# An encoder layer on one core: q stored in rows of 4 KB, the second chunk's tiles in another order, and VectorE's list of the first wave rearranged

## The chip, the cores and the metric

The kernel runs on one core of one Trainium2 chip. The metric is device microseconds for one execution. Everything is float32; matrix products keep their accuracy by splitting each operand into a high and a low half (type fp32r) and adding three products.

## The reference

One transformer layer with window attention and a dense feed-forward part, for one sequence of 2048 tokens and 1024 features:

```python
mod = silu(c) @ ada_w + ada_b                # 48 tiles of 128 values
sh1, sc1, g1, sh2, sc2, g2 = split(mod, 6)
h = rmsnorm(x, mix_norm_pre) * (1 + sc1) + sh1
q, k, v = split(h @ w_qkv)                   # 16 q heads, 4 k and v heads, 64 wide
logits = q @ k_band / 8 + rel_bias           # a block of 128 queries, 384 keys, |distance| <= 128
y = softmax([logits, sink])[..., :-1] @ v_band
x = x + g1 * rmsnorm(y @ w_o, mix_norm_post)
h = rmsnorm(x, ffn_norm_pre) * (1 + sc2) + sh2
a, b = split(h @ ffn_w_in)
x = x + g2 * rmsnorm((silu(a) * b) @ ffn_w_out, ffn_norm_post)
```

## The kernel before

**Chunks and tiles.** The tokens are cut into four chunks of 512. A chunk's x lies as eight tiles `x0` to `x7` of 128 features x 512 tokens (in the rows `x1_5` is chunk 1's tile 5). From them come a norm (`squares`, `norm`) and, for each k of eight, a scaling (`scale`, L207, written over x) and the two halves of `h` (`halves`: the high half on ScalarE, L214, the low half on VectorE, L215). The eight x buffers are shared, so a chunk's x tile is loaded when the low half of the chunk before it is done. The twelve output tiles of a chunk are numbered 0 to 7 for q, 8 and 9 for k, 10 and 11 for v; each is 24 matmuls (8 k, three products by the helper `three`, L145 to L147) of 128 x 512 into one of eight PSUM buffers. `NORD = [8, 9, 0, 1, 2, 3, 4, 10, 11, 5, 6, 7]` is their order in the weights: the first seven (`NORD[:WAVE]`) read the weight slices `w1`, the last five `w2`.

**The first wave** computes chunk 0's first seven tiles together, k by k, as the weights arrive. For each k VectorE has two adaLN products (`ada_reduce`, L297: a 128 x 1024 tile of `ada_w` times the conditioning vector, summed; tile 8+k gives the scale for x, tile k the shift for h), the low half of a weight slice (L151), a scaling and a low half of h. `squares0` squares chunk 0's x on ScalarE and adds pairs on VectorE; TensorE sums the four that are left over the partitions (`nsta`, L121). `tc.issue_after(...)` bounds from when on the scheduler may place what stands under it.

**Chunk 0's rest and chunk 1.** Then come the two v tiles (`psv`) and q tiles 5 to 7 of chunk 0, which read `w2` (loaded by `w_piece(k, 1)` through four raw buffers, cast on ScalarE, split on GpSimd), the norm of chunk 1 after the v tiles (`nsta`, L127, from the halves `nhla`, which take a buffer that the v tiles' stores give back), and chunk 1's twelve tiles. `late_ada` loads the 24 adaLN tiles that the attention doesn't need yet and reduces them between these. `evac` empties a q tile: high half on ScalarE (L229), low half on VectorE (L230), and for two tiles four DMA stores to the DRAM tensor `q_d` (L235), issued on ScalarE's queue for chunks 0 and 1 and on SP's after that. Loads and other stores are issued by SP, in order.

**Attention** has 64 units of 128 queries and four heads. `load_qkv` fetches q, k and v of a chunk and a k/v head. A unit has four score products (`s`, L497; the 128 x 128 piece of q is the weight operand, loaded anew for each of the two halves of k), the softmax on VectorE, ScalarE and GpSimd, transpositions (`t`, L519) and products with v. Chunks 2 and 3's projections and the output projection fill TensorE between the units. The memory of `w1`, `w2` and the raw buffers is used again for q, k, v and the softmax, from its beginning on: q, k and v lie where `w1` was.

**Feed-forward.** The hidden values come in pairs of blocks, whose sums and differences `give_pair` makes and stores; in the second half they are split before they are stored (`parted`). Instructions are ordered by a scheduler that has a timeline model; code order and `issue_after` guide it.

Of the kernel before, what the change touches and what calls it, by code (L numbers as in the profile page):

```python
# [10 lines left out]
F32 = mybir.dt.float32  # L11
F32R = mybir.dt.float32r
AF = mybir.ActivationFunctionType
ALU = mybir.AluOpType
# [3 lines left out]
P = 128  # L18
# [4 lines left out]
NCH = S // CH  # L23
NB = S // P
JB = CH // P
HEADS = 16
KVH = 4
GRP = 4
DH = 64
# [10 lines left out]
QW = P // GRP  # L40
# [4 lines left out]
NORD = [8, 9, 0, 1, 2, 3, 4, 10, 11, 5, 6, 7]  # L45
WAVE = 7
# [16 lines left out]
def f(ap):  # L63
    return ap.bitcast(F32)
# [3 lines left out]
def encoder_layer(ctx, tc, a):  # L68
# [9 lines left out]
    const = open_pool(ctx, "const")  # L78
    dram = open_pool(ctx, "dram", space=DRAM)

    q_d = [[dram.tile([P, JB * GRP, P], F32, name=f"q_d{c}_{g}") for g in range(KVH)] for c in range(NCH)]
    k_d = [[dram.tile([P, 2, CH], F32, name=f"k_d{c}_{g}") for g in range(KVH)] for c in range(NCH)]
    v_d = [[dram.tile([P, JB, P], F32, name=f"v_d{c}_{g}") for g in range(KVH)] for c in range(NCH)]
    o_d = [[dram.tile([P, KT, P], F32, name=f"o_d{c}_{b}") for b in range(JB)] for c in range(NCH)]
# [83 lines left out]
    class Chunk:  # L168
# [20 lines left out]
        def squares0(self):  # L189

            sq = [ev.tile([P, GRP, CH], F32, tag="eq", name=f"nsq0_{i}", bufs=2) for i in range(2)]
            sq = [sq[k // GRP][:, k % GRP] for k in range(KT)]
            for k in range(KT):
                act.activation(sq[k], self.xt[k], AF.Square)
                if k % 2:
                    dve.tensor_tensor(sq[k - 1], sq[k - 1], sq[k], ALU.add)
            self.acc = sq[::2]

        def norm(self, psp, ptag):
            self.r = rstd_of(lambda name: square_at(), psp, ptag, self.acc, f"a{self.c}", normed[:, 3])  # L200
# [18 lines left out]
    def evac(c, n, ps, psp, ptag):  # L219

        if n < KT:
            g, e = n // 2, n % 2
            if (c, g) not in pairs:
                pairs[c, g] = ev.tile([P, 2, JB * GRP, 2, QW], F32R, tag="eq", name=f"eq{c}_{g}", bufs=2)
            t = pairs[c, g]

            hi, lo = (t[:, i, :, e, :].rearrange("p (b s) r -> p b s r", b=JB) for i in range(2))
            src = ps.rearrange("p (b t) -> p b t", t=P)[:, :, ::-1].rearrange("p b (s r) -> p b s r", r=QW)
            act.activation(hi, src, AF.Copy, scale=DH ** -0.5)  # L229
            newest["evac"] = dve.scalar_tensor_tensor(lo, src, DH ** -0.5, f(hi), ALU.mult, ALU.subtract).ins  # L230
            pairs[c, g, e] = True
            if (c, g, 1 - e) in pairs:
                for j in range(2):
                    for i in range(2):
                        (act if c < 2 else sp).dma_start(q_d[c][g][i * DH:(i + 1) * DH, :, 2 * j * QW:2 * (j + 1) * QW],  # L235
                                     f(t[j * DH:(j + 1) * DH, i]).rearrange("p b e r -> p b (e r)"))
            return
        t = ev.tile([P, 2, CH], F32R, tag="e", name=f"e{c}_{n}")
        if n < KT + 2:
            split(t[:, 0], t[:, 1], ps, dve)  # L240
            for j in range(2):
                for d in range(2):
                    sp.dma_start(k_d[c][2 * (n - KT) + j][d * DH:(d + 1) * DH], f(t[j * DH:(j + 1) * DH]))
        else:
            vt = ev.tile([P, CH], F32, tag="vt", name=f"vt{c}_{n}", bufs=1)
            act.copy(vt, ps)
            pv = psp.tile([P, CH], F32, tag=ptag, name=f"pvt{c}_{n}")
            for j in range(JB):
                pe.transpose(pv[:, j * P:(j + 1) * P], vt[:, j * P:(j + 1) * P], ident)
            t = t.rearrange("p a b -> p (a b)").rearrange("p (g j i d) -> p g j i d", g=2, j=JB, i=2)  # L250
            s = pv.rearrange("p (j g d) -> p g j d", j=JB, g=2)
            for g in range(2):
                act.copy(t[:, g, :, 0, :], s[:, g])
                dve.tensor_tensor(t[:, g, :, 1, :], s[:, g], f(t[:, g, :, 0, :]), ALU.subtract)
                sp.dma_start(v_d[c][2 * (n - KT - 2) + g], f(t[:, g].rearrange("p j i d -> p j (i d)")))


    with ExitStack() as pa:
# [32 lines left out]
        def ada_load(t, pl):  # L291
            w = pl.tile([P, D], F32, tag="raw", name=f"ada{t}")
            sp.dma_start(w, a["ada_w"][t])
            return t, w

        def ada_reduce(t, w):
            dve.tensor_tensor_reduce(w, w, cb, 1.0, adab[:, t:t + 1], ALU.mult, ALU.add, mod[:, t:t + 1])  # L297
# [21 lines left out]
        for k in range(KT):  # L319
            with tc.issue_after(steps[max(k - 2, 0)][0]) if k >= 1 else ExitStack():  # L320
                ada_reduce(*ada_load(8 + k, raws))
                ada_reduce(*ada_load(k, raws))
                w_piece(k, 0)
            dve.scalar_tensor_tensor(coef[:, 0, k:k + 1], mod[:, 8 + k:9 + k], 1.0, gains[:, 0, k:k + 1],
                                     ALU.add, ALU.mult)
            with tc.issue_after(steps[k - 2][1]) if k >= 2 else ExitStack():
                steps.append(ch0.h(k))
            for n in NORD[:WAVE]:
                three(pss[n], wres[k, n], ch0.hh[k], k == 0, k == KT - 1)
        for n in NORD[:WAVE]:  # L330
            evac(0, n, pss[n], psA, "mm")
        wave.close()
        raws = open_pool(pa, "raws", 4, side="right")
        w2 = open_pool(pa, "w2", side="right")
        for k in range(KT):
            w_piece(k, 1)
        ch1 = Chunk(1)
# [42 lines left out]
        for i, n in enumerate(NORD[WAVE:]):  # L380
            qkv_tile(ch0, n)
            if i == 1:
                ch1.norm(psA, "mm")
            if i >= 1:
                ch1.h(2 * i - 2)
                ch1.h(2 * i - 1)
            if i >= 2:
                late_ada(min(i - 1, 2), 2)
        for i, n in enumerate(NORD[WAVE:] + NORD[:WAVE]):
            qkv_tile(ch1, n)  # L390
            late_ada(2, 2 if left else 0)
            if i == 0:
                ch2 = Chunk(2)
                ch2.squares()
            if i == 5:
                ch2.norm(psA, "mm")
            if 7 <= i < 11:
                ch2.h(2 * i - 14)
                ch2.h(2 * i - 13)
            if i == 0:  # L400

                with tc.issue_after(newest["split"]):
                    for r, h in enumerate(ROWS):
                        pool.dma_start(nsink[r * QW:(r + 1) * QW],
                                       bass.AP(tensor=a["sink"].tensor, offset=a["sink"].offset + h, ap=[[0, QW], [GRP, KVH]]))
                pool.tensor_scalar(nsink, nsink, -1.0, 1.0, ALU.mult, ALU.mult)
                rb = ev.tile([NBUCK + 1, HEADS], F32, tag="rb", name="rb", bufs=1)
                oh = ev.tile([P, CH], F32, tag="vt", name="oh", bufs=1)[:NBUCK + 1, :RLEN]
                tb = oh[:HEADS]
                pool.memset(rb, 1.0)  # L410
                with tc.issue_after(newest["split"]):
                    pool.dma_start(rb[:NBUCK], a["rel_bias"])
                    pool.dma_start(oh, a["onehot"])
                pst = psA.tile([P, CH], F32, tag="mm", name="pst")
                pe.matmul(pst[:HEADS, :RLEN], rb, oh, start=True, stop=True)
                act.copy(tb, pst[:HEADS, :RLEN])
                sp.dma_start(tab_d, tb)
# [36 lines left out]
    loaded = {}  # L454

    def load_qkv(c, g):
        q = qkv.tile([P, JB * GRP, P], F32R, tag="q", name=f"q{c}_{g}")
        sp.dma_start(f(q), q_d[c][g])
        kk = qkv.tile([P, 2, 6 * P], F32R, tag="k", name=f"k{c}_{g}")
        v = qkv.tile([P, 6, P], F32R, tag="v", name=f"v{c}_{g}")  # L460
        if c > 0:
            sp.dma_start(f(kk[:, :, :P]), k_d[c - 1][g][:, :, CH - P:])
            sp.dma_start(f(v[:, 0]), v_d[c - 1][g][:, JB - 1])
        sp.dma_start(f(kk[:, :, P:P + CH]), k_d[c][g])
        sp.dma_start(f(v[:, 1:1 + JB]), v_d[c][g])
        if c < NCH - 1:
            sp.dma_start(f(kk[:, :, P + CH:]), k_d[c + 1][g][:, :, :P])
            sp.dma_start(f(v[:, 1 + JB]), v_d[c + 1][g][:, 0])
        loaded[c, g] = (q, kk, v)

    class Unit:
# [10 lines left out]
        def scores(self):  # L482
# [9 lines left out]
            for i, (lo, hi) in enumerate(spans):  # L492
                n = hi - lo
                ps = psS.tile([P, CH], F32, tag="s", name=f"s{u}_{i}")
                qs = q[:, jb * GRP + i, :]
                for e in range(2):
                    m = pe.matmul(ps[:, :n], qs, kk[:, e, jb * P + lo:jb * P + hi], start=e == 0, stop=e == 1)  # L497
                    if i == e == 0:
# [401 lines left out]
    def give_pair(hf, j):  # L900
# [15 lines left out]
        if (hf, part_of[hf][j][0]) == LAST:  # L916
            for n in b:
                give(n, b[n], False)
            return
        b11, b12, b21, b22 = (b[n] for n in ("b11", "b12", "b21", "b22"))  # L920
        give("b11", b11, True)
        pool.tensor_tensor(b11, b12, b11, ALU.subtract)
        dve.tensor_tensor(b12, b22, b12, ALU.subtract)
        give("t3", b12, False)
        give("b22", b22, True)
        pool.tensor_tensor(b22, b22, b11, ALU.subtract)
        give("t1", b11, False)
        give("b21", b21, True)
        dve.tensor_tensor(b21, b21, b22, ALU.subtract)
# [419 lines left out]
```

## Time and profile before

| | |
|---|---|
| median of 3 runs | 2104.68 us (2103.5 to 2110.62) |
| profiled execution | 2106.09 us, span 2104.3 us |
| busy share of the span | TensorE 96%, VectorE 73%, ScalarE 48%, GpSimd 46% |
| chain that ended last | TensorE 72%, VectorE 10%, DMA 7%, GpSimd 4%, ScalarE 3% |
| DMA packets | 257286, of which under 512 B 84661 |

The span runs from the first to the last instruction; the execution's own time includes what lies around it. Busy shares are means over stages with different limits, so a stage has to be looked at by itself.

### The profile page before, as it was taken

To read this page: it belongs to the slowest core of one execution; us is meant where nothing else is said; L and a number is where in the kernel's file an instruction comes from. 1 tells how busy PE (TensorE), PEld (TensorE's weight loads), DVE (VectorE), ACT (ScalarE), POOL (GpSimd) and SP (SyncE) were. 2 spreads that over 40 slices of the span, in tenths; PEclk is the share of its full clock that TensorE was granted. 3 is DMA by queue.
4 is the path that set the end of the run, shared out by engine and by line. 5 is a ranking of instruction groups with operands and counts; after the bars stand their busy time and mean duration, and the time that the engine had idled before them with its cause. 6 is when DMAs were issued, how large, how long until landed. Compare 5 with 4: busy or idle time off the path is not lost.

```text
span 2104.3 us, 28775 instructions
## 1 busy us (share of the span) xinstructions
PE 2019.6 (96%) x9416; PEld 1663.9 (79%) x9416; DVE 1528.5 (73%) x2621; ACT 1005.2 (48%) x2129; POOL 969.4 (46%) x934
## 2 busy tenths in 40 slices
PE   8797899999999998999999999999999999999998
PEld 6676787888888786888888887888888788877886
DVE  8376677667777668576676698777875689987667
ACT  4233577776777756333333344434333654435222
POOL 0412446543445535455665455555453242395340
PEclk9899999999999999999999999999999999999999
DMA  8689668565555675443743454534434454469763
GB/s 313 189 281 284 185 184 263 175 166 182 168 187 202 212 241 187 140 129 118 247 158 108 160 177 151 196 140 178 162 145 160 151 196 135 135 249 365 264 243 128
DMA packets 257286, 402.69 MB, mean 191 GB/s; under 512 B 84661, under 2 KB 135397, under 8 KB 255088
## 3 DMA queue, kind: packets, MB, share of 16 engines
q1 hardware_dynamic: 216592, 371.41, 52.3%
q10 hardware_dynamic: 39072, 25.18, 3.9%
q0 software_dynamic: 1472, 4.27, 0.5%
q8 instruction: 74, 1.21, 0.2%
q14 instruction: 76, 0.62, 0.1%
HBM read 267.83 MB, written 132.95 MB: 190 GB/s over the span
## 4 chain that ended last, share of the span: by engine, by line
PE 72%; DVE 10%; DMA 7%; POOL 4%; issue 3%; ACT 3%; SPq 0%; DVEq 0%; ACTq 0%; POOLq 0%
PE pc_i L147 12%; PE pc_i L145 12%; PE pc_i L146 12%; PE po L1202 4%; PE po L1203 4%; PE po L1201 4%; PE t L519 3%; PE psq L146 2%; PE psq L147 2%; PE psq L145 2%; PE s L497 2%; PE py L613 2%; PE py L614 2%; PE py L615 2%; PE o L525 2%
## 5 line engine op out<-in xcount | busy, mean ns | idle before, releaser
L146 PE MATMUL pc_i<-ht,ws_i 128*128 128x512 f32 x528 | 207.5, 393 | 1.6 <-DVE ht L151 1.6
L145 PE MATMUL pc_i<-ht,ws_i 128*128 128x512 f32 x528 | 206.5, 392 | 1.6 <-ACT ht L150 1.6
L147 PE MATMUL pc_i<-ht,ws_i 128*128 128x512 f32 x528 | 207.4, 393 | 0.0
L150 ACT CAST wa_i<-wiri 128x512 fp32r<-128x512 f32 x132 | 81.7, 620 | 212.6 <-PE pc_i L147 121.6
L506 POOL TENSOR_SCALAR pr<-pr,rs 128x288 f32<-128x288 f32 (+3 forms) x256 | 125.4, 509 | 117.7 <-DVE rs L504 108.0
L502 ACT ACTIVATE pr<-pr,nm 128x289 f32<-128x289 f32 (+3 forms) x256 | 135.3, 530 | 58.5 <-DVE nm L500 57.0
L500 DVE CUSTOM_DVE_ANT_0 pr<-s,bias,nsink 128x288 f32<-128x288 f32 (+3 forms) x256 | 124.0, 500 | 53.4 <-PE s L497 41.9
L878 POOL TENSOR_TENSOR s_i<-wiri 128x512 f32<-128x512 f32 x44 | 61.3, 1394 | 193.1 <-DMA wiri<-w_in 146.1
L151 DVE TENSOR_TENSOR ws_i<-s_i,ws_i 128x512 fp32r<-128x512 f32 x132 | 126.7, 960 | 24.1 <-ACT ws_i L150 23.9
L151 DVE TENSOR_TENSOR wa_i<-wiri,wa_i 128x512 fp32r<-128x512 f32 x132 | 125.2, 948 | 20.2 <-ACT wa_i L150 19.7
L145 PE MATMUL pc_i<-hb,wa_i 128*128 128x512 f32 x352 | 139.0, 395 | 0.5 <-DVE u_i L945 0.5
L151 DVE TENSOR_TENSOR plo<-t,phi 128x512 fp32r<-128x512 f32 x184 | 121.8, 683 | 24.1 <-ACT phi L150 24.0
L146 PE MATMUL pc_i<-hb,wa_i 128*128 128x512 f32 x352 | 138.2, 393 | 0.0
L147 PE MATMUL pc_i<-hb,wa_i 128*128 128x512 f32 x352 | 138.2, 393 | 0.0
L1201 PE MATMUL po<-wo_s,g 128*128 128x512 f32 x320 | 125.2, 395 | 5.9 <-ACT wo_s L150 5.3
L1202 PE MATMUL po<-wo_s,g 128*128 128x512 f32 x320 | 126.0, 394 | 1.8 <-DVE wo_s L151 1.8
L497 PE MATMUL s<-k,q 128*128 128x288 f32 (+4 forms) x512 | 110.4, 314 | 17.1 <-DMA k<-k_d 11.0
L1203 PE MATMUL po<-wo_s,g 128*128 128x512 f32 x320 | 125.7, 393 | 0.0
L519 PE MATMUL t<-ident,pr 128*128 128x128 f32 x736 | 116.2, 275 | 6.6 <-POOL pr L506 5.8
L146 PEld LDWEIGHTS pc_i<-ht,ws_i 128*128 128x128 f32 x528 | 99.7, 189 | 23.9 <-DVE ht L151 2.1
L145 PEld LDWEIGHTS pc_i<-ht,ws_i 128*128 128x128 f32 x528 | 99.9, 189 | 23.5 <-ACT ht L150 2.0
L150 ACT CAST ws_i<-s_i 128x512 fp32r<-128x512 f32 x132 | 81.6, 618 | 75.7 <-PE pc_i L147 71.1
(253 smaller groups left out, 6037.5 us busy)
## 6 DMA issues: line engine op xcount, KB each, us to landing
wiri<-w_in SPq DMA_DIRECT2D x88, 512.0 KB, 4.0
ada<-ada_w SPq DMA_DIRECT2D x40, 512.0 KB, 6.7
wr<-w_out SPq DMA_DIRECT2D x20, 1024.0 KB, 9.1
g<-g_d_t SPq DMA_DIRECT2D x36, 512.0 KB, 5.6
g<-g_d_b SPq DMA_DIRECT2D x35, 512.0 KB, 5.3
q<-q_d SPq DMA_DIRECT2D x16, 1024.0 KB, 6.6
wsr<-w_qkv SPq DMA_DIRECT2D x24, 512.0 KB, 4.9
g<-g_d_t SPq DMA_DIRECT2D x44, 256.0 KB, 3.2
```

Of the source, the lines that this page charges most:

```text
L145: pe.matmul(ps, w[0], h[0], start=first, stop=False)
L146: pe.matmul(ps, w[0], h[1], start=False, stop=False)
L147: pe.matmul(ps, w[1], h[0], start=False, stop=last)
L150: act.copy(hi, src)
L151: return eng.tensor_tensor(lo, src, f(hi), ALU.subtract).ins
L497: m = pe.matmul(ps[:, :n], qs, kk[:, e, jb * P + lo:jb * P + hi], start=e == 0, stop=e == 1)
L502: act.activation(pr[:, i, lo:hi + 1], pr[:, i, lo:hi + 1], AF.Exp, bias=nm[:, i:i + 1], scale=-1.0, accum_out=rs[:, i:i + 1])
L506: pool.tensor_scalar(pr[:, i, lo:hi], pr[:, i, lo:hi], rs[:, i:i + 1], 1.0, ALU.mult, ALU.mult)
L519: pe.transpose(pt[:, i * P:(i + 1) * P], pr[:, i, jj * P:(jj + 1) * P], ident)
L1201: pe.matmul(ps, g[:, 0], w[:, 0], start=k == 0, stop=False)
L1202: pe.matmul(ps, g[:, 0], w[:, 1], start=False, stop=False)
L1203: pe.matmul(ps, g[:, 1], w[:, 0], start=False, stop=k == m - 1)
```

## The change

It has five parts. (1) `q_d` keeps, for each partition, the 128 rows of a head pair's dimensions times 16, so that a store writes 4 KB in one run for a partition, where it wrote 16 runs of 256 B. The eviction writes that order by reading PSUM with a step, and the score product reads its piece of q with a step of 16 elements. (2) Chunk 1 computes its tiles in chunk 0's order, and three late adaLN tiles are loaded beside each (and 2, 2, 3 beside chunk 0's last). (3) In the first wave the product for the shift is put behind the scaling of the tile before, and the square sums are added in fours, so TensorE sums two. (4) The memory of `w2` and of the raw buffers changes places. (5) In the parted pairs GpSimd's two subtractions go to VectorE.

```diff
-    q_d = [[dram.tile([P, JB * GRP, P], F32, name=f"q_d{c}_{g}") ...
+    q_d = [[dram.tile([P, P, JB * GRP], F32, name=f"q_d{c}_{g}") ...
...
                 if k % 2:
                     dve.tensor_tensor(sq[k - 1], sq[k - 1], sq[k], ALU.add)
-            self.acc = sq[::2]
+                if k % 4 == 3:
+                    dve.tensor_tensor(sq[k - 3], sq[k - 3], sq[k - 1], ALU.add)
+            self.acc = sq[::4]
...
-            hi, lo = (t[:, i, :, e, :].rearrange("p (b s) r -> p b s r", b=JB) for i in range(2))
-            src = ps.rearrange("p (b t) -> p b t", t=P)[:, :, ::-1].rearrange("p b (s r) -> p b s r", r=QW)
+            hi, lo = t[:, 0, e], t[:, 1, e]
+            src = ps.rearrange("p (n r) -> p n r", r=QW)[:, :, ::-1].rearrange("p n r -> p r n")
...
-                        (act if c < 2 else sp).dma_start(q_d[c][g][i * DH:(i + 1) * DH, :, 2 * j * QW:2 * (j + 1) * QW],
-                                     f(t[j * DH:(j + 1) * DH, i]).rearrange("p b e r -> p b (e r)"))
+                        (act if c < 2 else sp).dma_start(q_d[c][g][i * DH:(i + 1) * DH, j * DH:(j + 1) * DH],
+                                     f(t[j * DH:(j + 1) * DH, i]).rearrange("p e r b -> p (e r) b"))
...
                 ada_reduce(*ada_load(8 + k, raws))
-                ada_reduce(*ada_load(k, raws))
+                shift = ada_load(k, raws)
                 w_piece(k, 0)
+            with tc.issue_after(steps[k - 1][1]) if k >= 1 else ExitStack():
+                ada_reduce(*shift)
...
+        w2 = open_pool(pa, "w2", side="right")
         raws = open_pool(pa, "raws", 4, side="right")
-        w2 = open_pool(pa, "w2", side="right")
...
-                late_ada(min(i - 1, 2), 2)
-        for i, n in enumerate(NORD[WAVE:] + NORD[:WAVE]):
+                late_ada(2 + (i == 4), 2)
+        for i, n in enumerate(NORD):
             qkv_tile(ch1, n)
-            late_ada(2, 2 if left else 0)
+            late_ada(3, 2 if left else 0)
...
-                qs = q[:, jb * GRP + i, :]
+                qs = q[:, :, jb * GRP + GRP - 1 - i]
...
+        eng = dve if parted else pool
         give("b11", b11, True)
-        pool.tensor_tensor(b11, b12, b11, ALU.subtract)
+        eng.tensor_tensor(b11, b12, b11, ALU.subtract)
...
-        pool.tensor_tensor(b22, b22, b11, ALU.subtract)
+        eng.tensor_tensor(b22, b22, b11, ALU.subtract)
```

The scheduler places the instructions anew. On VectorE, in the first wave (`x0_0`, `h0_0`: chunk 0's tile 0; `ada9`, `ada10` scales, `ada1` a shift, `w0_1` a weight slice), there stood before:

```order
L207 SCALAR_TENSOR_TENSOR x0_0_417<-x0_0_417,coef_365,normed_385 128x512
L297 ISA ada9_540,mod_358<-ada9_540,normed_385,adab_359 128x1024
...
L297 ISA ada1_543,mod_358<-ada1_543,normed_385,adab_359 128x1024
...
L151 TENSOR_TENSOR w0_1_548<-wqkv1_0_546,w0_1_548 128x896
L297 ISA ada10_577,mod_358<-ada10_577,normed_385,adab_359 128x1024
...
L215 SCALAR_TENSOR_TENSOR h0_0_516<-x0_0_417,mod_358,h0_0_516 128x512
...
L297 ISA ada2_580,mod_358<-ada2_580,normed_385,adab_359 128x1024
```

and now:

```order
L209 SCALAR_TENSOR_TENSOR x0_0_417<-x0_0_417,coef_365,normed_385 128x512
L299 ISA ada9_540,mod_358<-ada9_540,normed_385,adab_359 128x1024
...
L151 TENSOR_TENSOR w0_1_547<-wqkv1_0_545,w0_1_547 128x896
L299 ISA ada10_577,mod_358<-ada10_577,normed_385,adab_359 128x1024
...
L217 SCALAR_TENSOR_TENSOR h0_0_516<-x0_0_417,mod_358,h0_0_516 128x512
L299 ISA ada1_543,mod_358<-ada1_543,normed_385,adab_359 128x1024
...
L151 TENSOR_TENSOR w0_2_584<-wqkv2_0_582,w0_2_584 128x896
```

The product for `ada1` has gone behind the low half `h0_0`.

On SP, at the loads of the second weight slices (`wqkv0_1` to `wqkv7_1`; `x1_4` to `x1_7` are chunk 1's x tiles, `k_d0` the stores of chunk 0's k), there stood before:

```order
L175 DMA x1_4_885<-xT 128x512
L304 DMA wqkv0_1_841<-w_qkv 128x640
...
L304 DMA wqkv3_1_856<-w_qkv 128x640
L175 DMA x1_5_886<-xT 128x512
L175 DMA x1_6_887<-xT 128x512
L175 DMA x1_7_888<-xT 128x512
L304 DMA wqkv4_1_861<-w_qkv 128x640
...
L304 DMA wqkv6_1_871<-w_qkv 128x640
L304 DMA wqkv7_1_876<-w_qkv 128x640
```

and now:

```order
L175 DMA x1_4_885<-xT 128x512
L175 DMA x1_5_886<-xT 128x512
L175 DMA x1_6_887<-xT 128x512
L306 DMA wqkv0_1_841<-w_qkv 128x640
...
L306 DMA wqkv3_1_856<-w_qkv 128x640
L175 DMA x1_7_888<-xT 128x512
L306 DMA wqkv4_1_861<-w_qkv 128x640
...
L306 DMA wqkv6_1_871<-w_qkv 128x640
L245 DMA k_d0_0_76<-e0_8_799 64x1024 x2
...
L245 DMA k_d0_3_79<-e0_9_806 64x1024 x2
L306 DMA wqkv7_1_876<-w_qkv 128x640
```

All x tiles but `x1_7` now stand ahead of the first slice, and the k stores ahead of the last one.

On SP, at the end of chunk 1 (`x3` are chunk 3's x tiles, `q0_0`, `k0_0`, `v0_0` the first unit's loads), there stood before:

```order
L293 DMA ada35_1577<-ada_w 128x1024
L293 DMA ada36_1579<-ada_w 128x1024
L175 DMA x3_0_1922<-xT 128x512
...
L293 DMA ada37_1622<-ada_w 128x1024
...
L293 DMA ada39_1664<-ada_w 128x1024
...
L175 DMA x3_7_1929<-xT 128x512
L458 DMA q0_0_1796<-q_d0_0_60 128x2048
L464 DMA k0_0_1798<-k_d0_0_76 128x2x512
L465 DMA v0_0_1799<-v_d0_0_92 128x512
L467 DMA k0_0_1798<-k_d1_0_80 128x2x128
```

and now:

```order
L295 DMA ada38_1457<-ada_w 128x1024
L295 DMA ada39_1459<-ada_w 128x1024
L462 DMA q0_0_1796<-q_d0_0_60 128x2048
L468 DMA k0_0_1798<-k_d0_0_76 128x2x512
L469 DMA v0_0_1799<-v_d0_0_92 128x512
L471 DMA k0_0_1798<-k_d1_0_80 128x2x128
...
L462 DMA q0_1_1843<-q_d0_1_61 128x2048
...
L175 DMA x3_0_1922<-xT 128x512
...
L175 DMA x3_3_1925<-xT 128x512
```

The first unit's loads now stand ahead of chunk 3's x tiles, and follow the last adaLN load.

## Rows read from the trace of the kernel before

**Rows 1.** Windows: microseconds; busy time (instructions) by engine; clock; DMA share; GB/s.

```profile
20.00:40.00 20.00, 13.63 (x50) 10.18 (x50) 19.96 (x35) 7.14 (x9) 0.00 (x0) 0.91 1.03 406
...
120.00:140.00 20.00, 19.10 (x121) 17.40 (x122) 17.79 (x30) 5.49 (x11) 5.49 (x3) 0.91 0.89 279
...
200.00:220.00 20.00, 19.87 (x82) 16.16 (x83) 8.34 (x18) 8.72 (x20) 8.30 (x7) 0.89 0.84 229
...
260.00:760.00 500.00, 489.92 (x2674) 411.46 (x2673) 354.04 (x937) 361.27 (x924) 255.02 (x409) 1.00 0.61 190
...
1300.00:1600.00 300.00, 300.00 (x1318) 247.13 (x1317) 235.25 (x320) 122.06 (x213) 157.22 (x112) 1.00 0.45 163
```

**Rows 2.** TensorE's waits, 0 to 130: releaser, total, times, longest.

```profile
PE nsta L127 <- DVE nhla L125: 15.7, 1, 15.7
PE psq L146 <- DVE h L215: 5.6, 3, 2.6
PE psv L147 <- DVE h L215: 2.1, 1, 2.1
```

**Rows 3.** TensorE's waits, 130 to 260.

```profile
PE s L497 <- DMA k<-k_d: 11.0, 1, 11.0
PE t L519 <- POOL pr L506: 4.8, 1, 4.8
```

**Rows 4.** VectorE's groups, 20 to 60: busy, mean ns, idle before.

```profile
L297 DVE CUSTOM_DVE_ANT_0 ada<-ada,normed,adab 128x1024 f32<-128x1024 f32 x14 | 17.6, 1285 | 0.0
...
L151 DVE TENSOR_TENSOR w<-wqkv,w 128x896 fp32r<-128x896 f32 x7 | 7.6, 1093 | 0.0
L207 DVE SCALAR_TENSOR_TENSOR x<-x,coef,normed 128x512 f32<-128x512 f32 x8 | 6.0, 751 | 0.0
```

**Rows 5.** SP's queue, 40 to 75: start, length, what.

```profile
48.05 1.85 SPq L304 DMA_DIRECT2D wqkv<-w_qkv  x4
```

**Rows 6.** Tile `k_d`: duration ns min/median/max, first and last start.

```profile
L243 SPq DMA_DIRECT2D k_d<-e x32: 445/816/2324, 68.7 to 353.9; - x32
```

**Rows 7.** Tile `wqkv`: the split on GpSimd, and loads to landing.

```profile
L151 POOL TENSOR_TENSOR w<-wqkv,w x8: 1568/1796/2028, 57.2 to 71.0; 128x640 fp32r<-128x640 f32 x8
...
DMA to landing us min/median/max: 3.4/4.5/9.8
```

**Rows 8.** TensorE in order of time, at the second chunk's norm.

```profile
96.15 0.80 PE L127 MATMUL nsta<-nhla,ones 128*128 128x512 f32 x1 [15.68 <-DVE nhla L125]
```

**Rows 9.** ScalarE in order of time, 60 to 97.

```profile
70.41 6.88 ACTq L235 DMA_DIRECT2D q_d<-eq  x4
...
78.63 10.73 ACTq L235 DMA_DIRECT2D q_d<-eq  x4
89.40 0.27 ACT L358 CAST e_v<-psv 128x128 fp32r<-128x128 f32 x1 [11.47 <-DMA q_d<-eq]
```

**Rows 10.** Tile `q_d`: ScalarE's stores, duration ns min/median/max.

```profile
L235 ACTq DMA_DIRECT2D q_d<-eq x32: 515/1340/5160, 70.4 to 204.5; - x32
```

**Rows 11.** Chain of waits, 0 to 240: start, length, what.

```profile
92.36 3.19 DMA v_d<-e_v
...
193.89 6.11 DMA k<-k_d
...
221.56 7.52 DMA wsr<-w_qkv
```

**Rows 12.** TensorE in order of time, 500 to 516.

```profile
500.01 0.42 PE L497 MATMUL s<-k,q 128*128 128x288 f32 x2
...
507.68 0.38 PE L519 MATMUL t<-ident,pr 128*128 128x128 f32 x2
...
508.14 0.93 PE L519 MATMUL t<-ident,pr 128*128 128x128 f32 x7
...
513.75 0.69 PE L497 MATMUL s<-k,q 128*128 128x288 f32 x4
```

**Rows 13.** Line 922, the pairs' first subtraction.

```profile
L922 POOL TENSOR_TENSOR p_i<-u_i,p_i x20: 1288/1294/1742, 833.5 to 1575.3; 128x512 f32<-128x512 f32 x20
```

More of the change, by code (lines that the diff above doesn't have):

```diff
@@ L79, in encoder_layer @@
     dram = open_pool(ctx, "dram", space=DRAM)
-    q_d = [[dram.tile([P, JB * GRP, P], F32, name=f"q_d{c}_{g}") for g in range(KVH)] for c in range(NCH)]
+    q_d = [[dram.tile([P, P, JB * GRP], F32, name=f"q_d{c}_{g}") for g in range(KVH)] for c in range(NCH)]
     k_d = [[dram.tile([P, 2, CH], F32, name=f"k_d{c}_{g}") for g in range(KVH)] for c in range(NCH)]
@@ L223, in evac @@
             if (c, g) not in pairs:
-                pairs[c, g] = ev.tile([P, 2, JB * GRP, 2, QW], F32R, tag="eq", name=f"eq{c}_{g}", bufs=2)
+                pairs[c, g] = ev.tile([P, 2, 2, QW, JB * GRP], F32R, tag="eq", name=f"eq{c}_{g}", bufs=2)
             t = pairs[c, g]
-            hi, lo = (t[:, i, :, e, :].rearrange("p (b s) r -> p b s r", b=JB) for i in range(2))
-            src = ps.rearrange("p (b t) -> p b t", t=P)[:, :, ::-1].rearrange("p b (s r) -> p b s r", r=QW)
+            hi, lo = t[:, 0, e], t[:, 1, e]
+            src = ps.rearrange("p (n r) -> p n r", r=QW)[:, :, ::-1].rearrange("p n r -> p r n")
             act.activation(hi, src, AF.Copy, scale=DH ** -0.5)
@@ L456, in load_qkv @@
     def load_qkv(c, g):
-        q = qkv.tile([P, JB * GRP, P], F32R, tag="q", name=f"q{c}_{g}")
+        q = qkv.tile([P, P, JB * GRP], F32R, tag="q", name=f"q{c}_{g}")
         sp.dma_start(f(q), q_d[c][g])
```

## The prediction

> **What bounds the kernel now.** I read the windows first. TensorE is busy 489.92 of 500 us in the attention stage and all of 300 us in the feed-forward stage [rows 1], so there an edit counts only if it gives TensorE more to do, or stops it. The holes are in the first 260 us. The waits of TensorE in 0 to 130 us name three: 15.7 us before the norm of the second chunk (`nsta`, L127), 5.6 us in three pieces in the first wave (the low half of `h`, L215), 2.1 us in the second chunk's first tiles [rows 2]. From 130 to 260 us there are 11.0 us before the first scores (`k` from DRAM) and 4.8 us before a transposition [rows 3]. After the 11.0 us the granted clock averages 0.89 over 20 us [rows 1], so some of that work runs at the lower of its two levels.
>
> **The first wave: little by itself.** VectorE is busy 19.96 of 20 us there [rows 1]: 14 adaLN products of 1285 ns, seven weight splits of 1093 ns, eight scalings of 751 ns and eight low halves of about the same [rows 4]. The change reorders these; their sum stays, apart from two adds of square sums ahead of the norm. The first low half comes one product (1.3 us) earlier, and TensorE's waits shrink. A stage that VectorE fills ends when VectorE has done its list; of the 5.6 us I take 4, and the next part shows why they are not cashed.
>
> **Second weight slices: a new wait.** In the before kernel the first four loads of `w2` are issued at 48.05 us [rows 5]. In the new order they stand on SP behind `x1_5` and `x1_6`, which overwrite x tiles of chunk 0 and so wait for the low halves of k = 5 and 6, where `x1_4` waited for k = 4. That is two rounds of VectorE's list, each of two products, a split, a scaling and a low half: 2 x 1.285 + 1.093 + 2 x 0.751 = 5.2 us. With the 4 us that the wave is ahead they are issued near 48 + 10.4 - 4 = 54.5. The last slice's load moves behind eight `k` stores, which are issued in 0.816 us each [rows 6], 6.5 us in all; and ScalarE casts slices 6 and 7 after eight q stores. A load lands 4.5 us after its issue, and GpSimd splits a slice in 1.796 us [rows 7]. From about 60 us on eight splits take 14.4, and the gap before slice 6 some 5 more: the last low half is there near 80 us. The two v tiles are 96 matmuls of 256 columns, of which 44 stand ahead of those that read slice 7. The other 52, at half of the 300 / 1318 = 0.228 us of one with 512 columns [rows 1], are 5.9 us: the v tiles end near 86.5, where they now end at 96.15 - 15.68 = 80.5 [rows 8].
>
> **q stores in rows of 4 KB: what the norm gains.** ScalarE's queue is held 6.88 and 10.73 us by two groups of four q stores, and the casts of v wait 11.47 us behind the second [rows 9]. A store of 64 partitions has 64 x 16 runs of 256 B; afterwards it has 64 runs of 4 KB, the shape of a `k` store: 0.816 us [rows 6] where a q store on ScalarE takes a median of 1.340 and up to 5.160 [rows 10]. Eight take about 6.5 instead of 17.6 us, and end before the v tiles do. After these still come the last casts and subtractions (some 1.3 us), the v store, 3.19 us [rows 11], which frees the buffer that `nhla` is written into, and the cast of `nhla`, 1 us with its start. So `nsta` starts near 86.5 + 5.5 = 92 in place of 96.15: **minus 4 us**. Bounds: minus 13 if the slices come in time (the wave's 4 us cashed, v tiles end at 77), plus 3 if the stores stay slow.
>
> **Second chunk in the first's order, more adaLN beside.** From `nsta` on TensorE's work is the same, but before the chunk's first low half VectorE has one product more (1.285 us), and TensorE a little less to fill with. The wait of 2.1 us becomes 3.7: **plus 1.6**. All 24 late tiles are reduced as before, three beside a tile instead of two; VectorE is busy 17.79 of 20 us at its densest there [rows 1] and TensorE runs up to seven tiles ahead in PSUM, so I cost the denser loads at nothing. If that cover is gone it is the third rival.
>
> The gain is at the end of the stage. The loads of q, k and v for the first scores go over the memory of the first weight slices, which were read last and are now read by the chunk's first seven tiles; and on SP they stand ahead of chunk 3's x loads instead of behind. They can be issued five tiles, some 5 x 24 x 0.228 = 27 us, before the scores. The chain of waits shows 6.11 us from the load of `k` to the scores [rows 11]; the whole wait of 11.0 us goes: **minus 11.0**. With it goes the slow clock behind it, 0.11 of 20 us: **minus 2.2**. The 4.8 us come from a late load of streamed weights (7.52 us in the chain [rows 11]), whose cast on ScalarE holds up the softmax; SP has less queued up then: **minus 4.8**, bounds 0 and minus 8.
>
> **Strided reads.** The q weights of 512 score matmuls are afterwards read at a step of 64 B, and the eviction reads PSUM at a step of 128 B. No row has either. For the eviction: nothing to twice the time, 0.6 us more on ScalarE and on VectorE for each of 32 tiles; both wait for TensorE there, so nothing on the path. For the weights: transpositions, each with a load of 128 columns, come (0.93 - 0.38) / 5 = 0.11 us apart, score matmuls (0.69 - 0.42) / 2 = 0.135 us [rows 12]. So a load fits into 0.11 us now, hidden behind 0.135. At no penalty it costs nothing. At half speed, 0.22 us, each of the 256 second matmuls of a pair is 0.09 us late, 23 us, and so are some 146 first ones that follow a score or a transposition in the new order, 13 us: 36. I take nothing: a load reads an element in 0.11 / 128 = 0.86 ns, while the moving operand is read in 0.228 / 512 = 0.45 ns, so the weight reader is far from the fastest that these rows show.
>
> [...]
>
> **The feed-forward edit.** Two subtractions of nine pairs in the second half go from GpSimd (1.294 us each [rows 13]) to VectorE. At that price 18 of them are 23 us, in a stage where TensorE has no hole and VectorE is busy 235.25 of 300 [rows 1]. Nothing; if VectorE became late there, a few us.
>
> **The sum.** The profiled execution took 2106.1 us (span 2104.3), 1.4 over the median of 2104.7. 2106.1 - 4 + 1.6 - 11.0 - 2.2 - 4.8 = 2085.7: **2086 us**, its own range 2075 to 2097.
>
> **Rivals.** (1) *Strided weights at half speed.* 36 us exceed the gain of 20.4: 2122, slower. It decides from 20.4 / 402 = 0.05 us on each exposed load. For it: no element shares a neighbourhood with the next; against: the slow pace above. 0.16. (2) *The second weight slices come in time,* since the DMA is freed of small packets and loads land sooner than their median: `nsta` at 83, 9 us more, 2077. For it: the DMA is full now (share 1.03 in the wave [rows 1]); against: the order on SP. 0.12. (3) *The wait moves.* Three adaLN loads a tile beside x loads and stores fill the DMA; VectorE stands in an adaLN product, evictions and chunk 2's norm queue behind it, and two thirds of the 11.0 and 4.8 us come back as such waits: 2097, or 2102 with all. For it: a DMA share of 0.89 already [rows 1]; against: the short packets in that share go. 0.14. (4) The forecast: 0.58.
>
> A measurement of this kernel tells a difference of about 0.3%, 6.3 us, from no change. Faster (below 2098.4) are the forecast, rival 2 and 0.02 of rival 3: 0.72. The same: the rest of rival 3, and 0.02 of rival 1 for a penalty of some 20 us: 0.14. Slower: the rest of rival 1, 0.14. The range, 2070 to 2110, leaves out most of rival 1 and a little below.
>
> **What would show it.** Right: no long wait before `s`; q stores on ScalarE under 1 us; v tiles that wait for `w2` from GpSimd between 65 and 85 us, and `nsta` near 92; score matmuls still 0.135 us apart. Wrong: score matmuls 0.2 us apart (rival 1); no wait in the v tiles (rival 2); VectorE idle before adaLN products from 100 to 190 us (rival 3).

## The result, and the profile after

The changed kernel takes 2125.85 us (median of 5 runs, 2119.68 to 2127.57) where the kernel before, beside it, takes 2105.74: a ratio of 1.0085 with a 95% interval of 1.0064 to 1.0107. It is **slower**, by 0.85%, some 18 to 20 us, and the interval lies wholly above 1. The forecast was 2086, with a range of 2070 to 2110; what came is nearest to the first rival, the strided weights (2122). That its number is so near is partly luck: the runs below put the strided weights at 23 to 28 us, not 36, and the rest of the change gained 5 to 8 us, not 20.4, so that two errors nearly cancel.

First TensorE's waits in the changed kernel, 0 to 130 us and then 130 to 260 us (releaser; total, times, longest):

```profile
PE psv L145 <- ACT w L150: 12.4, 2, 10.5
PE psq L146 <- DVE h L217: 6.6, 4, 3.3
PE nsta L127 <- DVE nhla L125: 4.0, 1, 4.0
PE psv L146 <- POOL w L151: 2.1, 3, 0.8
...
PE psq L145 <- ACT ws L150: 3.6, 1, 3.6
PE s L501 <- DVE eq L232: 1.8, 1, 1.8
```

Against [rows 2, 3]: the 15.7 us before the norm have become 4.0, but 14.5 us of waits for `w`, the second weight slices, stand in the v tiles; the 11.0 us for `k` and the 4.8 before a transposition are gone, and 1.8 and 3.6 us have come. By this list alone the kernel should be a little faster. The windows show where it isn't:

```profile
20.00:40.00 20.00, 18.35 (x77) 13.79 (x76) 19.96 (x34) 7.45 (x11) 0.00 (x0) 1.00 1.03 406
80.00:100.00 20.00, 10.87 (x60) 9.79 (x60) 3.03 (x9) 4.07 (x11) 6.62 (x9) 0.67 0.66 219
...
200.00:220.00 20.00, 18.34 (x78) 14.92 (x79) 10.19 (x31) 12.85 (x32) 17.68 (x22) 0.86 0.94 268
260.00:760.00 500.00, 494.47 (x2559) 429.55 (x2557) 339.65 (x904) 348.53 (x891) 249.39 (x401) 1.00 0.58 182
1300.00:1600.00 300.00, 298.15 (x1302) 245.09 (x1301) 244.15 (x339) 121.61 (x211) 139.31 (x95) 0.99 0.45 161
```

In the 500 us of attention TensorE is busier than in [rows 1] (494.47, was 489.92) and gets through fewer instructions: 2559 matmuls, where it did 2674. No wait shows this; the instructions have become longer. The score line of the changed kernel, and of the kernel before (duration in ns, least, median and most; first and last start):

```profile
L501 PEld LDWEIGHTS s<-k,q x512: 291/303/334, 197.0 to 750.5; 128*128 128x128 f32 x171
```

```profile
L497 PEld LDWEIGHTS s<-k,q x512: 186/188/338, 200.1 to 731.6; 128*128 128x128 f32 x171
```

A load of q weights takes 303 ns instead of 188. The first score starts 3.1 us earlier than before and the last one 18.9 us later: the stage from the first to the last is 553.5 us long, was 531.5. In TensorE's order of time the spacing can be read:

```profile
214.06 0.96 PE L501 MATMUL s<-k,q 128*128 128x288 f32 x4
218.78 0.52 PE L501 MATMUL s<-k,q 128*128 128x288 f32 x2
```

Two more matmuls take 0.44 us more, so they are 0.22 us apart, where [rows 12] gave 0.135. That is the sign that the prediction named for rival 1.

The norm of the second chunk, to be held against [rows 8]:

```profile
101.11 0.80 PE L127 MATMUL nsta<-nhla,ones 128*128 128x512 f32 x1 [3.95 <-DVE nhla L125]
```

The profiled execution is 2125.0 us long (span), 20.7 more than before. By its landmarks: the norm starts at 101.1 instead of 96.15 (+5.0); from there to the first score it is 95.9 instead of 104.0 us (-8.1); from the first to the last score +22.0; from there to the end +1.8.

### The profile page after: what moved, and what is told of

Its sections match the earlier page's. It is cut to its first block, busy times and chain, and to the rows that moved or that the text cites. A ratio compares the mean times of both kernels' runs of the same rounds, so it can differ in the third digit from the quotient of the medians.

```text
span 2125.0 us, 28757 instructions
## 1 busy us (share of the span) xinstructions
PE 2052.2 (97%) x9412; PEld 1706.5 (80%) x9412; DVE 1529.2 (72%) x2641; ACT 1005.7 (47%) x2129; POOL 956.0 (45%) x916
## 5 line engine op out<-in xcount | busy, mean ns | idle before, releaser
L501 PE MATMUL s<-k,q 128*128 128x288 f32 (+4 forms) x512 | 148.7, 389 | 4.7 <-DVE nm L504 3.0
L151 DVE TENSOR_TENSOR wa_i<-wiri,wa_i 128x512 fp32r<-128x512 f32 x132 | 137.7, 1043 | 21.3 <-ACT wa_i L150 21.1
L501 PEld LDWEIGHTS s<-k,q 128*128 128x128 f32 x512 | 130.4, 305 | 14.3 <-DVE nm L504 6.3
L151 DVE TENSOR_TENSOR ws_i<-s_i,ws_i 128x512 fp32r<-128x512 f32 x132 | 116.6, 883 | 23.2 <-ACT ws_i L150 23.0
```

The source lines that it names most:

```text
L151: return eng.tensor_tensor(lo, src, f(hi), ALU.subtract).ins
```

## The experiments

Ratios are to the kernel before, on the same chip, with 95% intervals. "Norm" is the start of the second chunk's `nsta`.

### The step of the score weights

**after_step1**, **after_step2** and **after_step4** change only the elements that the score product reads as weights, to a step of one, two and four; every instruction stands where it stood.

```diff
-                qs = q[:, :, jb * GRP + GRP - 1 - i]
+                qs = q.rearrange("p a b -> p (a b)")[:, (jb * GRP + i) * P:(jb * GRP + i + 1) * P]
```

> The changed kernel, but the score product takes its 128 columns of q weights side by side (step of one element) and not 64 B apart; it multiplies other elements of the same tile of q, so the output is not that of the layer, and every instruction stands where it stood. Theory S (the weight load at a step of 64 B is slower, its price shows where a load is not covered by a longer matmul): weight loads of the scores back from 303 to 188 ns, score matmuls 0.135 us apart, and 22 to 36 us less than the changed kernel, 2090 to 2104 us. Theory O (the strided load is hidden, the loss comes from the new order of the loads, tiles and VectorE's list): weight loads shorter but the time within 5 us of the changed kernel, 2120 to 2128 us.

> The changed kernel with the score weights read at a step of 8 B (two elements); other elements of the same tile of q are multiplied, so the output is not that of the layer. [...] Theory S2 (any step of more than one element costs): weight loads near 303 ns, time that of the changed kernel, 2120 to 2128 us. Theory O: no difference in time either way.

> The changed kernel with the score weights read at a step of 16 B (four elements); other elements of the same tile of q are multiplied, so the output is not that of the layer. [...] Rival (the price grows with the distance): between 200 and 290 ns, 2102 to 2118 us.

Measured: 2097.46 us at step one (0.9975, 0.9956 to 0.9994); 2099.58 at step two and 2138.23 at step four, one run each. The weight loads, in that order:

```profile
L501 PEld LDWEIGHTS s<-k,q x512: 186/188/333, 198.1 to 726.1; 128*128 128x128 f32 x171
```

```profile
L501 PEld LDWEIGHTS s<-k,q x512: 192/196/332, 196.6 to 728.3; 128*128 128x128 f32 x171
```

```profile
L501 PEld LDWEIGHTS s<-k,q x512: 307/311/337, 200.5 to 757.6; 128*128 128x128 f32 x171
```

Theory S holds and O falls: the step alone costs 28 us by the medians, 23 by the ratios, and 25 us in the length from first to last score (553.5 against 528.0). And the price doesn't grow with the step: 8 B are nearly free (196 ns), 16 B cost all (311) and 64 B no more (303). So S2 falls at 8 B, by load and by time (2099.58 us, where step one takes 2097.46), and the rival of after_step4 at 16 B, where the load is above its 200 to 290 ns and the one run above its 2102 to 2118 us. Why the price sets in between 8 and 16 B no run shows.

### The layout of q alone, and all but the layout

**before_rows** puts only part 1 into the kernel before; **after_old_q** takes only part 1 out of the changed one.

> The kernel before with the layout of q alone changed (rows of 4 KB, eviction and score weights read at a step). Theory S: the attention stage is 22 to 36 us longer, some of the 15.7 us before the norm of the second chunk goes; 2117 to 2137 us. Theory O: the shorter stores gain and the strided load is hidden: 2095 to 2106 us.

> The changed kernel with the old layout of q (runs of 256 B, contiguous reads and weights), all other parts of the change kept. Theory S: the strided weights go and the slow stores come back; the casts of the last slices of w2 wait longer behind the q stores, so the norm of the second chunk starts at 104 to 110 us, not 101.1; altogether 2092 to 2108 us. Theory O: 2120 us or more.

Measured: before_rows 2127.59 us (1.0113, 1.0091 to 1.0134), as S said. Its norm starts at 92.35, 3.8 us earlier, and its first score at 192.7, 7.4 us earlier, before the strided weights take it back: from first to last score it is 557.7 us, 26 longer than in the kernel before.

```profile
92.35 0.79 PE L127 MATMUL nsta<-nhla,ones 128*128 128x512 f32 x1 [12.18 <-DVE nhla L125]
```

```profile
L497 PEld LDWEIGHTS s<-k,q x512: 291/304/330, 192.7 to 750.4; 128*128 128x128 f32 x171
```

after_old_q was a miss: 2119.47 us (1.0064, 1.0047 to 1.0081), close to O's number, though its weight loads take 188 ns. Its waits, 60 to 215 us, and one that follows right after the first scores:

```profile
PE psv L145 <- ACT w L150: 14.8, 1, 14.8
PE s L501 <- DVE eq L232: 8.1, 1, 8.1
PE nsta L127 <- DVE nhla L125: 4.0, 1, 4.0
...
PE psq L145 <- ACT ws L150: 11.3, 1, 11.3
```

So the new order has a loss of its own, which the 4 KB rows soften: the v tiles wait for `w`, the first score for the last eviction of q (1.8 us in the changed kernel), and then a projection tile for the cast of `ws`, the weights of the later chunks (3.6 there). With that last wait in it, the stretch from first to last score is 541.4 us.

### The moved product

**no_shift** puts the product for the shift back beside that for the scale, in the changed kernel. **no_shift_step1** also reads the weights side by side. **before_wave** puts part 3 alone into the kernel before.

```diff
-                shift = ada_load(k, raws)
+                ada_reduce(*ada_load(k, raws))
...
-            with tc.issue_after(steps[k - 1][1]) if k >= 1 else ExitStack():
-                ada_reduce(*shift)
```

> The changed kernel with the product for the shift back beside that for the scale (one edit of part 3 undone); this puts the loads and casts of the second weight slices back ahead of the x tiles, the k stores and the q stores. Theory T (the moved product is what puts those loads and casts late, and the v tiles stop for them): the 12.4 us of waits in the v tiles fall under 3, the norm of the second chunk starts at 88 to 93 us and not at 101.1, and the time falls by 8 to 16 us to 2110 to 2118. Theory U (the stores themselves hold ScalarE and SP, wherever the casts stand): the wait goes to the norm, which starts at 98 us or later, and the time stays at 2120 or more.

> The kernel no_shift with the score weights read side by side (other elements of q, so the output is not that of the layer): the change without its two faults. If the two prices add: 2118.6 less 28 gives 2088 to 2093 us, with the norm at 93 us and the first scores at 191 us. If the time that the strided weights take hides waits that come back without them: 2095 us or more.

> The kernel before with part 3 alone: the product for the shift behind the scaling of the tile before, and square sums in fours. Prediction's terms (the wave ends 4 us earlier, the second weight slices come later): v tiles with 8 to 15 us of waits, here behind q stores of 256 B, norm of the second chunk at 98 to 106 us and not at 96.15, time 2 to 8 us over the kernel before. Rival (the wait before the norm was there anyway, so the v tiles only wait in its place): norm within 1 us of 96.15, time within 2 us.

Measured: no_shift 2118.56 us (1.0075, 1.0055 to 1.0095), no_shift_step1 2094.91 (0.9959, 0.9944 to 0.9974), before_wave 2119.01 (1.008, 1.0067 to 1.0094). TensorE's waits of no_shift, and then of before_wave, 60 to 215 us:

```profile
PE nsta L127 <- DVE nhla L125: 12.9, 1, 12.9
PE s L499 <- DVE eq L232: 3.8, 1, 3.8
```

```profile
PE psv L145 <- ACT w L150: 15.2, 1, 15.2
PE s L501 <- DMA k<-k_d: 10.7, 1, 10.7
PE nsta L127 <- DVE nhla L125: 4.0, 1, 4.0
```

T holds for the waits: without the moved product no v tile waits and the norm starts at 93.1; with part 3 alone, in the kernel before, the v tiles wait 15.2 us in one piece and the norm starts at 101.7. It does not hold for the time. In the changed kernel the moved product costs 2 us by the ratios, 7 by the medians (6 at the last score of the profiles), where T said 8 to 16, and the two intervals overlap, so no cost is shown. In the kernel before part 3 costs 17 us, where 2 to 8 were expected. There 5.5 us come at the norm, and some 9.5 us more in the attention stage (first to last score 541.0 us), in many small waits for the softmax. Why these grow I did not find. no_shift_step1 is between its two expectations; against no_shift the step of the weights costs 24 us here too.

### The second chunk's order alone

**before_chunk1** puts parts 2 and 4 into the kernel before.

> The kernel before with the second chunk's tiles in the first's order, three late adaLN tiles beside each, and the two memory pools exchanged; q's layout, the wave and the feed-forward part stay. Prediction's term (the 11.0 us before the first scores, the 2.2 of slow clock and the 4.8 before a transposition go): 2084 to 2092 us. Rival (the wait moves: the last q tile's eviction now stands behind q stores of 256 B on ScalarE, as two runs showed with 8 to 19 us before the first scores): first scores at 200 us or later, 2098 to 2108 us.

Measured: 2110.71 us (1.0039, 1.0022 to 1.0056): the rival, and a little above its range. TensorE's waits, 190 to 230 us, and ScalarE in order of time:

```profile
PE s L497 <- DVE eq L230: 11.7, 1, 11.7
PE psq L145 <- ACT ws L150: 11.6, 1, 11.6
```

```profile
193.95 5.18 ACTq L235 DMA_DIRECT2D q_d<-eq  x2
199.26 0.60 ACT L229 ACTIVATE eq<-psq 128x512 fp32r<-128x512 f32 x1 [4.92 <-issue]
...
208.32 8.51 ACTq L235 DMA_DIRECT2D q_d<-eq  x4
216.87 1.04 ACT L150 CAST ws<-wsr 128x1024 fp32r<-128x1024 f32 x1 [14.09 <-DMA v<-v_d]
```

In this order the chunk's last evictions of q, and the cast of `ws`, stand behind q stores of 256 B on ScalarE, just where the first scores and the next projection tile wait for them: 11.0 us for `k` have become 11.7 for `eq` and 11.6 for `ws`. With 4 KB rows the same order costs 3.8 and 2.5 (no_shift): parts 1 and 2 belong together. no_shift is 9 us faster than before_rows by the medians, 8 by the ratios, but it has part 5 as well, which alone gave 4.

### Where the short runs are

Can the stores be short without the strided weights? **before_pairs** and **no_shift_pairs** interleave pairs of blocks (runs of 512 B, a step of 8 B, the eviction in two halves). **pairs_gpsimd** issues the latter's q stores of chunks 0 and 1 on GpSimd's queue.

```diff
+    q_d = [[dram.tile([P, JB * GRP // 2, P, 2], F32, name=f"q_d{c}_{g}") ...
+                qs = q[:, ix // 2, :, ix % 2]
...
-                        (act if c < 2 else sp).dma_start(q_d[c][g][...
+                        (pool if c < 2 else sp).dma_start(q_d[c][g][...
```

> The kernel before with that layout of q alone (runs of 512 B, step of 8 B). If half-long runs are as good as rows of 4 KB: the 23 us by which the rows alone were slower become a gain, 2094 to 2101 us, the norm of the second chunk at 92 us. If runs of 512 B are no better than 256 B: 2101 to 2108 us, norm at 96 us.

> The kernel no_shift with another layout of q: pairs of blocks interleaved, so that runs are 512 B and the score weights have a step of 8 B; the eviction is cut in two for it. Theory S with T: the 28 us of the strided weights go as well, 2080 to 2094 us, the score weight loads near 196 ns. Rival: 512 B runs hold ScalarE as runs of 256 B did and the norm waits again until 96 us or later, 2095 to 2106 us.

> The kernel no_shift_pairs with the q stores of chunks 0 and 1 issued on GpSimd's queue and not on ScalarE's. If ScalarE's queue, held by stores, is what delays the casts of v (14.3 us before the norm) and the last eviction (18.6 us before the first scores): norm at 83 to 90 us, first scores at 180 to 192 us, 2076 to 2092 us. Rival (the stores are late by the DMA itself, whatever queue issues them): the wait goes over to the loads of q and k, 2095 us or more.

Measured: before_pairs 2111.55 us (1.0039, 1.0022 to 1.0057), no_shift_pairs 2099.80 (0.9991, 0.9979 to 1.0002), pairs_gpsimd 2134.03 (1.0155, 1.013 to 1.0179). Half-long runs don't cure the queue: the norm starts at 95.2 and 95.3, and before the first score there are 10.0 us (for `eq`) and 18.6 us, in no_shift_pairs with the eviction again behind stores. Some 7 us of the 18.6 come after these stores: the later pieces of the eviction, up to 206.9, stand between other work on ScalarE. no_shift_pairs, ScalarE in order of time:

```profile
193.80 5.75 ACTq L239 DMA_DIRECT2D q_d<-eq  x4
199.68 0.40 ACT L231 ACTIVATE eq<-psq 128x256 fp32r<-128x256 f32 x1 [11.08 <-DMA v_d<-e_v]
```

On GpSimd's queue the casts of v are free and the norm starts at 88.9, but the stores themselves come one every 3.4 to 7 us, though for most of them the engine waits for nothing that the profile shows (`issue`), and the first score waits until 219.1. The norm is where the first expectation put it, the time where the rival did. GpSimd in order of time:

```profile
79.59 0.70 POOL L239 DMA_DIRECT2D q_d<-eq  x1 [3.69 <-issue]
86.33 0.65 POOL L239 DMA_DIRECT2D q_d<-eq  x1 [6.03 <-issue]
90.70 0.66 POOL L239 DMA_DIRECT2D q_d<-eq  x1 [3.73 <-issue]
```

**before_late_runs** and **no_shift_late_runs** store rows of 4 KB, as two halves, and have the runs of 256 B in the load of q on SP's queue; the weights lie side by side.

```diff
+    q_d = [[dram.tile([P, 2, JB * GRP, DH], F32, name=f"q_d{c}_{g}") ...
+                        (act if c < 2 else sp).dma_start(q_d[c][g][i * DH:(i + 1) * DH, j],
+        for j in range(2):
+            sp.dma_start(f(q[:, :, j * DH:(j + 1) * DH]), q_d[c][g][:, j])
```

> The kernel before with that storage of q alone: 4 KB stores, 256 B runs in the loads, weights side by side. If the held queue is what the rows cure: norm at 92 us and first scores at 193 us as in before_rows, without its strided weights, 2094 to 2101 us. If the number of short packets is what costs: 2102 us or more, the 11.0 us before the first scores longer than before.

> The kernel no_shift with q stored in rows of 4 KB as in the change, but kept there as two halves, so that the load of q into SBUF has the runs of 256 B and the score weights lie side by side: the short runs are moved from the stores on ScalarE's queue to the loads on SP's. If ScalarE's held queue is what the rows cure: norm at 93 us, first scores near 191 us, weight loads 188 ns, 2088 to 2096 us, as the run no_shift_step1. If the number of short packets is what costs, wherever they are: first scores at 200 us or later, or waits for q in the attention stage, 2100 us or more.

Measured: before_late_runs 2098.55 us (0.9983, 0.9969 to 0.9997), norm at 93.95: the held queue was a cost. But its wait for `k` is still 9.8 us, where before_rows waited 6.5: on SP's queue the q loads with short runs, two for each tile of q, take a median of 1.220 us each, in before_rows the one load of a tile takes 0.330. no_shift_late_runs was a miss: 2104.48 us (1.0008, 0.9995 to 1.0021), norm at 93.2, first score at 195.1 behind a wait of 7.1 us for `eq`, and a stage from first to last score of 542.0 us that I can't account for. The time is where the rival put it (2100 or more), but neither of the rival's signs is there: the first scores come before 200, and no wait for q stands in the attention stage.

### The feed-forward edit, and a version that is faster

**before_ffn** puts part 5 alone into the kernel before; **before_late_ffn** is before_late_runs with part 5.

> The kernel before with the two subtractions of the parted pairs on VectorE alone. Prediction's term: no difference, within 3 us of the kernel before. Rival (a few us of late casts on VectorE): 2107 to 2112 us.

> The kernel before with two edits that were each a little faster alone: q stored in rows of 4 KB with the short runs in the loads (0.9983 of the kernel before), and the two subtractions of the parted pairs on VectorE (0.9979). If they add, being in different stages: 0.996, 2094 to 2098 us. If not: 2098 to 2102 us.

Measured: before_ffn 2100.72 us (0.9979, 0.9964 to 0.9993), 4 us faster: less than the 6.3 that the prediction took for the least difference, but the interval lies below 1. before_late_ffn 2096.04 us (0.9969, 0.9956 to 0.9981) is the fastest that computes the layer, faster than both kernels; the product of its two ratios (0.9962) lies in its interval, so the two may well add.

## Why the prediction was wrong, point by point

- **Strided reads: "I take nothing".** This step failed. The argument was that a load reads an element in 0.86 ns and the moving operand in 0.45, so the reader has room. It has none at a step of 64 B: the load went from 188 to 303 ns, and the change lost 23 to 28 us by it, more than the 20.4 it was to gain. Rival 1's slower strided load and its 0.22 us were right; its 36 us were some 10 too many; whether the 13 us in it for the first matmuls of a pair were too much, or other waits shrank, was not tried apart. That rival deserved more than 0.16, as the row used against it showed contiguous reads only.
- **The eviction from PSUM** at a step of 128 B is free: 598 and 686 ns in the changed kernel, for 597 and 691 before:

```profile
L231 ACT ACTIVATE eq<-psq x32: 576/598/629, 67.2 to 467.3; 128x512 fp32r<-128x512 f32 x32
...
L232 DVE SCALAR_TENSOR_TENSOR eq<-psq,eq x32: 654/686/694, 68.7 to 468.6; 128x512 fp32r<-128x512 f32 x32
```

- **Second weight slices: "the v tiles end near 86.5".** The wait was foreseen, its size was not: the last matmul that waits for a slice starts at 89.1 and the v tiles end at 97.2. The first four loads are issued at 56.1, forecast 54.5; 0.9 us of that is a row misread, since the eight low halves are not "about the same" as the scalings (751 ns) but 1177 ns in the kernel before:

```profile
L215 DVE SCALAR_TENSOR_TENSOR h<-x,mod,h 128x512 fp32r<-128x512 f32 x8 | 9.3, 1177 | 0.0
```

  SP and then ScalarE in the changed kernel:

```profile
56.12 1.85 SPq L306 DMA_DIRECT2D wqkv<-w_qkv  x4
...
62.44 3.39 SPq L306 DMA_DIRECT2D wqkv<-w_qkv  x3
68.18 11.99 SPq L245 DMA_DIRECT2D k_d<-e  x8
80.28 1.09 SPq L306 DMA_DIRECT2D wqkv<-w_qkv  x1
```

```profile
69.98 11.45 ACTq L237 DMA_DIRECT2D q_d<-eq  x7
81.47 0.60 ACT L231 ACTIVATE eq<-psq 128x512 fp32r<-128x512 f32 x1 [11.62 <-DMA q_d<-eq]
81.97 0.72 ACT L150 CAST w<-wqkv 128x640 fp32r<-128x640 f32 x1
86.72 0.72 ACT L150 CAST w<-wqkv 128x640 fp32r<-128x640 f32 x1 [4.03 <-DMA wqkv<-w_qkv]
```

  Both groups of eight stores took 12.0 us, where the prediction had 6.5 from `k_d`'s median of 0.816 us [rows 6]. That is a median over the whole stage; here sixteen stores are issued on two queues at once. SP's queue in the kernel before has a row for this very place, beside q stores of 256 B:

```profile
68.69 12.53 SPq L243 DMA_DIRECT2D k_d<-e  x8
```

  So slice 6 is cast at 81.97, behind q stores, and slice 7 is loaded at 80.28, behind k stores. In the wait the clock falls (0.50 from 82 to 92 us, 0.67 from 80 to 100), and the last matmuls take 8 us for 5.9.
- **"Minus 4 us" at the norm** became +5.0. 4 KB rows by themselves do give about what was taken (before_rows: norm at 92.35), but not by the way that was taken: eight q stores hold ScalarE 13.2 us there, 17.6 before, and not 6.5, and the v tiles, without a wait, end at 80. The moved product takes the gain away and 5 more. The lower bound of minus 13 was not there to be had: with slices in time (no_shift) the norm is at 93.1, not 83, after a wait of 12.9 us.
- **The wave** went nearly as forecast: it ends 3.2 us earlier, of 4 (65.81 instead of 69.03), and that isn't cashed.
- **"Plus 1.6" in the second chunk:** the wait for the first low half is 3.3 us, forecast 3.7.
- **"Minus 11.0, minus 2.2, minus 4.8".** The waits named did go, and from the norm to the first score 8.1 us were gained, of 9.4 forecast (11.0 less 1.6); but 5.4 us came back as waits for ScalarE's eviction and cast. The mean clock from 200 to 220 us did not rise (0.86, was 0.89); from 190 to 260 it did (0.95, was 0.88; the lower of its two levels, in the kernel before from 194 to 204 us, is 0.50). But the term was credited to the order of the tiles, and alone that order is worth nothing (before_chunk1: +0.4%): what stands behind the q stores there was not looked at, as rival 3 looked at adaLN loads and not at ScalarE. Its own sign is not there: VectorE waits 1.2 us for adaLN loads from 100 to 190 us.
- **The feed-forward edit: "nothing"** was 4 us, a gain (before_ffn). The price of 1.294 us was GpSimd's; on VectorE one takes 0.69 us in the changed kernel. Where the gain comes from is not shown.
- **The sum** without the strided weights: 2097.5 us, a gain of some 5 to 8 us where 20 were forecast. no_shift_step1, with neither fault, is at 2094.9. So even with free strided reads the gain would have been less than half of the forecast. The norm, 9 us later than the 92 forecast, and the 5.4 us of waits that came back are about as much as is missing; but no_shift_step1, with its norm at 93.6, gains only 9 us by its ratio, so what takes the rest stays open.

## What to carry to other kernels

When a layout makes a transfer cheaper, price the reader first: 512 weight loads at a step of 64 B cost 23 to 28 us, and the wait that shorter stores were to shorten was 15.7. Price a group of DMA issues from a group under the same load, not from the median of a stage. And after moving one instruction, look at what now stands behind the stores on each queue: here one product on VectorE put two weight slices behind sixteen stores.

## What the runs showed of the hardware that was not expected

Weights at a step of 16 B load a little slower than at 64 B (311 against 303 ns; the kernels 2138.23, one run, against 2125.85). The longer load accounts for some 4 of these 12 us (first to last score 557.1 against 553.5). A q store on GpSimd's queue occupies it for 0.65 us, yet the next is issued 3.4 to 7 us later (pairs_gpsimd). And the attention stage from first to last score varies from 525.5 us (no_shift_pairs, 207.8 to 733.3) to 542.0 (no_shift_late_runs) among kernels whose weight loads take 188 or 196 ns, for the most part by small waits (one long wait, 11.3 and 11.6 us for `ws`, is in after_old_q, 541.4, and before_chunk1, 537.5); that stays open.
